# Attention: reciprocal softmax sums of a head turned in one transpose and re-read from memory as rows

## The chip, the cores and the metric

The kernel runs on one core of a Trainium2 chip. The metric is device time in microseconds (us) of one execution, the median of the runs. The core has five engines with queues of their own that run in order: PE (matmuls, and PEld for its weight loads), DVE, ACT, POOL, and SP, which here only issues DMAs. They meet through semaphores; a scheduler places each engine's instructions from the order in which the program issues them and from priorities.

## What is computed

A two-layer trunk over 1024 latent tokens and 256 context tokens. Each layer projects the tokens, runs three token mixers side by side (retention, grouped-query attention GQA with 6 heads, latent attention MLA with 6 heads), multiplies their concatenation by SiLU(gate), and projects back. Only the two attentions and the gate matter here:

```python
def one_block(qi):
    s = jnp.einsum('bqkgd,bskd->bkgqs', qi, k).astype(f32) * scale
    p = jax.nn.softmax(s, axis=-1).astype(v.dtype)
    return jnp.einsum('bkgqs,bskd->bqkgd', p, v)
```

Latent queries see 1536 keys, context queries 256. The kernel does not normalise the probabilities: it multiplies the head's output by the reciprocal of the row sum, and then by the gate.

## The kernel before, in words

The attention of a layer is one list of 60 *pairs*. A pair is (head `i`, token pair `pr`, mixer): 256 tokens of one head of GQA or MLA; pairs 0 to 3 of a head are latent tokens (three key blocks of 512), pair 4 is the context (one key block of 256). GQA runs ahead of MLA by `LEAD` = 3 pairs. Outputs stand transposed: a head's columns `head_cols` in `yxs` hold 64 GQA rows above 64 MLA rows on the partitions, and tokens along the free dimension.

`advance` is one step; in each it issues at most one job of each kind, with lags counted in steps, and `up(...)` gives each kind a priority:

- `s_job`: scores of 128 queries against one key block (PE, L1247, L1248, for MLA also L1250) into a bank "acc"; DVE takes the maximum (L1256).
- `exp_job`: ACT's exponential with the row sum (L1270). After a pair's last block DVE makes the reciprocal sums `ri`, one number for each token, tokens on partitions (L1277, L1278, for the context pair L1280).
- `t_job`: four PE transposes of the probabilities (L1288) into a bank "tp", then ACT rounds (L1292) and DVE takes the rest (L1293). There are two "tp" banks.
- `pv_job`: output matmuls (L1304, L1305) into the only bank "o". When a pair is done ACT copies half of it (L1316) and DVE adds (L1317) into `head_cols`, which releases the bank.
- `y_job`, once both halves of (`i`, `pr`) are done, 30 times a layer: POOL spreads `ri` over 256 columns (`rb`, one buffer, L1355), PE turns it by two transposes into a bank "tp" (L1358), DVE multiplies `head_cols` by that bank (L1359), POOL multiplies by the gate `gt` (L1360). `gt` is loaded by `load_gates` (L1335) when the first half of the pair is done. `gate_retention` (L1344, its load at L1347) gates the retention columns in head 1 and reads a load `gr` with one buffer.

Between the jobs POOL prepares what the next pairs need: `q_piece` splits queries in two terms (L1169, L1171), `qr_piece` the rotary part (L192, L193), and `step` splits the next head's K and V as their loads land (L192, L193). SP issues all loads in order: K and V rows (`st`, L1090, L1107, L1086), rotary queries (`qst`, L1180), gates (L1335).

Of the kernel before, what the change touches and what calls it, by code (L numbers as in the profile page):

```python
# [10 lines left out]
F32 = mybir.dt.float32  # L11
# [3 lines left out]
ALU = mybir.AluOpType  # L15
# [3 lines left out]
P = 128  # L19
# [4 lines left out]
DEPTH = 2  # L24
# [4 lines left out]
Y_H = 256  # L29
# [36 lines left out]
RB = 6  # L66
YV = 1
LEAD = 3
# [8 lines left out]
SV = 0  # L77
WG = 1
PO = 1


def hybrid_trunk(tc, I, O):
# [3 lines left out]
    V, A, G, T = nc.vector, nc.scalar, nc.gpsimd, nc.tensor  # L86
    dma = nc.sync.dma_start
# [6 lines left out]
    s_gT = [tc.dram_tile([D, NT * P], F32, name=f"s_gT{l}") for l in range(DEPTH)]  # L94
# [5 lines left out]
    s_mv = [tc.dram_tile([6 * P, NCH * 64], F32, name=f"s_mv{l}") for l in range(DEPTH)]  # L100
    s_kpT = [tc.dram_tile([NCH * 32, P], F32, name=f"s_kpT{l}") for l in range(DEPTH)]
    s_mt = [tc.dram_tile([P, 512], F32, name=f"s_mt{l}") for l in range(DEPTH)]
    s_gate = [tc.dram_tile([2, D], F32, name=f"s_gate{l}") for l in range(DEPTH)]


    cst = enter(tc.tile_pool(name="cst", reuse_waits="tile", bufs=1))
    wp = enter(tc.tile_pool(name="wp", reuse_waits="tile", bufs=4))
    wr = enter(tc.tile_pool(name="wr", reuse_waits="tile", bufs=1))
    sm = enter(tc.tile_pool(name="sm", reuse_waits="tile", bufs=4))
    pp = enter(tc.tile_pool(name="pp", reuse_waits="tile", bufs=1, space=PSUM))  # L110

    ident = cst.tile([P, P], F32, name="ident")
    dma(ident, I["ident"])
    yxs = cst.tile([P, NT, D], F32, name="yx")
# [19 lines left out]
    def bank(tag):  # L134
        if tag == "o":
            return pp.tile([P, 512], F32, name=tag, tag=tag, bufs=1)
        if tag == "m":
            tag = "tp"
        bufs = {"acc": NACC, "tp": 7 - NACC}[tag]
        return pp.tile([P, 512], F32, name=tag, tag=tag, bufs=bufs)  # L140

    def up(offset):
        return tc.high_priority(offset=offset) if offset else nullcontext()
# [297 lines left out]
    def phase_b(l, p1, acts, ws, first, first_side, first_done, att):  # L441
        pa_ctx = ExitStack()

        def blk(fn, pre=None, post=None, posts=1):
            gran, n = ws.take()
            if pre is not None:
                pre(0)
            for t in range(NT):
                if pre is not None and t + 1 < NT:
                    pre(t + 1)  # L450
                fn(t, project(act_of(acts, t), gran, n))
                if t in (0, 2, 4, 6):
                    ws.pump()
                for _ in range(posts):
                    next(post, None)
# [246 lines left out]
        blk(gqa_fn, post=side)  # L702
        blk(gqb_fn, post=side, posts=PO)
        for _ in side:
# [355 lines left out]
    def attention(l, att):  # L1060
# [3 lines left out]
        at = None  # L1064
# [175 lines left out]
        clock = [0]  # L1240
# [27 lines left out]
        def exp_job(p, i, b, ps):  # L1268
            pn = at.tile([P, 512], F32, name="pn", tag="pn", bufs=PN)[:, :p.w]
            A.activation(pn, ps, AF.Exp, bias=p.ng[i], accum_out=p.su[:, i, b:b + 1])  # L1270
            p.pn[i, b] = pn
            if b == p.nb - 1 and i == 1:
                if (p.i, p.pr) not in ris:
                    ris[p.i, p.pr] = sm.tile([P, 2, 2], F32, name="ri", tag="ri", bufs=RB)
                ri = ris[p.i, p.pr][:, :, p.mla]
                if p.nb > 1:
                    V.tensor_reduce(ri, p.su[:, :, 0:p.nb], axis=AX.X, op=ALU.add)  # L1277
                    V.reciprocal(ri, ri)  # L1278
                else:
                    V.reciprocal(ri, p.su[:, :, 0])  # L1280

        def t_job(p, i, b):
            if i == 0:
                p.gran[b] = at.tile([P, 2, 4, 256], F32R, name="pT", tag="pT", bufs=PT)
            pn = p.pn.pop((i, b))
            pt = bank("tp")
            for c in range(p.nch):
                T.transpose(pt[:, c * 128:(c + 1) * 128], pn[:, c * 128:(c + 1) * 128], ident)  # L1288
            p3 = pt[:, :p.w].rearrange("p (c q) -> p c q", c=p.nch)
            ph = p.gran[b][:, 0, 0:p.nch, i * 128:(i + 1) * 128]  # L1290
            pl = p.gran[b][:, 1, 0:p.nch, i * 128:(i + 1) * 128]
            A.copy(ph, p3)  # L1292
            V.tensor_tensor(pl, p3, ph.bitcast(F32), op=ALU.subtract)  # L1293

        def pv_job(p, b, c0, c1):
            if b == 0 and c0 == 0:
                p.po = bank("o")[:, :256]
            last = p.nb * p.nch - 1
            while (p.i not in MV) if p.mla else p.i // 3 not in GV:
                step(True)  # L1300
            for c in range(c0, c1):
                ch = b * p.nch + c
                vc = (MV[p.i] if p.mla else GV[p.i // 3])[:, p.k0 // 128 + ch, :]
                T.matmul(p.po, vc, p.gran[b][:, 0, c, :], start=(ch == 0), stop=False)  # L1304
                T.matmul(p.po, vc, p.gran[b][:, 1, c, :], start=False, stop=(ch == last))  # L1305
            if b == p.nb - 1 and c1 == p.nch:
                hs = slice(64 * p.mla, 64 * p.mla + 64)
                if YV == 0:
                    o2 = at.tile([P, 2, 256], F32, name="o2", tag="o2", bufs=OH)
                    for u in range(2):  # L1310
                        A.copy(o2[hs, u], p.po[64 * u:64 * u + 64])
                    o4 = o2[hs].rearrange("p a (t c) -> p a t c", t=2)
                    G.tensor_tensor(head_cols(p)[hs], o4[:, 0], o4[:, 1], op=ALU.add)
                else:
                    o2 = at.tile([P, 256], F32, name="o2", tag="o2", bufs=OH)
                    A.copy(o2[hs], p.po[64:128])  # L1316
                    V.tensor_tensor(head_cols(p)[hs], p.po[0:64].rearrange("p (t c) -> p t c", t=2),  # L1317
                                    o2[hs].rearrange("p (t c) -> p t c", t=2), op=ALU.add)
                pairs_done[p.mla] += 1
                halves[p.i, p.pr] = halves.get((p.i, p.pr), 0) + 1  # L1320
                if halves[p.i, p.pr] == 1:
                    load_gates(p)
                else:
                    ys.append((clock[0] + 1, p))

        def head_cols(p):

            return yxs[:, 2 * p.pr:2 * p.pr + 2, Y_H + p.i * 128:Y_H + (p.i + 1) * 128]

        ris, halves, gates = {}, {}, {}  # L1330

        def load_gates(p):

            gates[p.i, p.pr] = g = at.tile([P, 2, 128], F32, name="gt", tag="gt", bufs=LEAD + 1)
            dma(g, s_gT[l][(2 + p.i) * P:(3 + p.i) * P, 2 * p.pr * P:(2 * p.pr + 2) * P].rearrange("p (t c) -> p t c", t=2))  # L1335

        rets = []

# [10 lines left out]

        def y_job(p):  # L1350

            pm = bank("tp")[:, :256]
            ri = ris.pop((p.i, p.pr)).rearrange("p t s -> p (t s)")
            rb = at.tile([P, 256], F32, name="rb", tag="rb", bufs=1)
            G.tensor_scalar(rb.rearrange("p (x c) -> p x c", c=64), ri.unsqueeze(2).to_broadcast([P, 4, 64]), 1.0, 1.0,  # L1355
                            op0=ALU.mult, op1=ALU.mult)
            for i in range(2):
                T.transpose(pm[:, i * 128:(i + 1) * 128], rb[:, i * 128:(i + 1) * 128], ident)  # L1358
            V.tensor_tensor(head_cols(p), head_cols(p), pm.rearrange("p (t c) -> p t c", t=2), op=ALU.mult)  # L1359
            G.tensor_tensor(head_cols(p), head_cols(p), gates.pop((p.i, p.pr)), op=ALU.mult)  # L1360
            gate_retention(p)

        LAG_E, LAG_T, LAG_V = LE, LT, LV
# [1 line left out]
        def advance(jobs):  # L1365

            s = clock[0]
            if jobs is not None:
                with up(OS):
                    s_job(*jobs)  # L1370
            if exps and s >= LAG_E:
                with up(OE):
                    exp_job(*exps.pop(0))
            if trs and trs[0][0] <= s and (trs[0][2], trs[0][3]) in trs[0][1].pn:
                _, p, i, b = trs.pop(0)
                with up(OT):
                    t_job(p, i, b)
                if i == 1:
                    h = max(1, p.nch // HV)
                    pvs.append((s + LAG_V, p, b, 0, h))  # L1380
                    pvs.append((s + LAG_V + 1, p, b, h, p.nch))
            if pvs and pvs[0][0] <= s:
                with up(OV):
                    pv_job(*pvs.pop(0)[1:])
            if ys and ys[0][0] <= s:
                with up(OY):
                    y_job(ys.pop(0)[1])
            clock[0] += 1
# [3 lines left out]
        for x in range(30 + LEAD):  # L1392
            for mla, y in ((1, x - LEAD), (0, x)):
                if 0 <= y < 30:
                    p = Pair()
# [20 lines left out]
        for n, p in enumerate(pairs):  # L1416
# [7 lines left out]
            for u in range(2):  # L1424
                for b in range(p.nb):
                    if early[0] == 0:
                        yield "prepared"
                        at = att.ctx.enter_context(tc.tile_pool(name=f"at{l}", reuse_waits="tile", bufs=1))
# [21 lines left out]
        while exps or trs or pvs or ys:  # L1450
            advance(None)
# [241 lines left out]
```

## Time and profile before

| | us |
|---|---|
| median of 3 runs | 2163.35 (2161.07 to 2163.56) |
| profiled execution, its own time | 2162.85 |
| its span | 2161.1 |
| PE busy in it | 2084.2 (96%) |
| DVE, ACT, POOL busy | 1502.0, 1183.5, 978.2 |

The attention of the first layer fills the trace from about 520 to 998 us, that of the second from about 1562 to 2037 us. A busy share is an average over the whole span, and PE's instructions are pipelined: where PE streams, a row's time from start to start says what an instruction takes; the duration of one row (0.27 us for a single transpose) includes its way through the array.

### The profile page before, as it was taken

To read this page: it belongs to the slowest core of one execution; us is meant where nothing else is said; L and a number is where in the kernel's file an instruction comes from. 1 tells how busy PE (TensorE), PEld (TensorE's weight loads), DVE (VectorE), ACT (ScalarE), POOL (GpSimd) and SP (SyncE) were. 2 spreads that over 40 slices of the span, in tenths; PEclk is the share of its full clock that TensorE was granted. 3 is DMA by queue.
4 is the path that set the end of the run, shared out by engine and by line. 5 is a ranking of instruction groups with operands and counts; after the bars stand their busy time and mean duration, and the time that the engine had idled before them with its cause. 6 is when DMAs were issued, how large, how long until landed. Compare 5 with 4: busy or idle time off the path is not lost. (4 is left out here: it accounts for less than half of the span.)

```text
span 2161.1 us, 42292 instructions
## 1 busy us (share of the span) xinstructions
PE 2084.2 (96%) x14888; PEld 1870.0 (87%) x14888; DVE 1502.0 (70%) x3830; ACT 1183.5 (55%) x3180; POOL 978.2 (45%) x1444
## 2 busy tenths in 40 slices
PE   7999999999999999999999999998999999999998
PEld 3899987788888888888999999887788888888898
DVE  4625583666889999997174358546689899999824
ACT  3503333225788888886243233322488888888623
POOL 2341242315576465533543324233375656453474
PEclk8999999999999999999999999999999999999999
DMA  9542446414111010004143212452311111000322
GB/s 315 145 145 63 123 112 204 122 49 117 36 44 28 20 30 25 13 27 136 46 153 102 66 54 55 140 152 66 109 46 30 32 30 32 14 22 18 98 91 98
DMA packets 189117, 173.30 MB, mean 80 GB/s; under 512 B 35833, under 2 KB 171625, under 8 KB 188905
## 3 DMA queue, kind: packets, MB, share of 16 engines
q1 hardware_dynamic: 187464, 165.35, 25.7%
q10 hardware_dynamic: 1440, 5.24, 0.6%
q8 instruction: 119, 1.95, 0.4%
q14 instruction: 94, 0.76, 0.1%
HBM read 124.77 MB, written 45.76 MB: 79 GB/s over the span
## 5 line engine op out<-in xcount | busy, mean ns | idle before, releaser
L256 PE MATMUL acc<-wh,ah 128*128 128x256 f32 (+1 forms) x1760 | 503.4, 286 | 1.8 <-ACT ah L404 1.8
L258 PE MATMUL acc<-wh,al 128*128 128x256 f32 (+1 forms) x1760 | 500.6, 284 | 2.5 <-DVE al L405 2.4
L257 PE MATMUL acc<-wl,ah 128*128 128x256 f32 (+1 forms) x1760 | 502.7, 286 | 0.0
L1256 DVE TENSOR_REDUCE nm<-acc 128x1 f32<-128x512 f32 (+1 forms) x624 | 411.7, 665 | 39.0 <-PE acc L1250 27.0
L1293 DVE TENSOR_TENSOR pT<-tp,pT 128x512 fp32r<-128x512 f32 (+1 forms) x624 | 413.2, 664 | 36.1 <-ACT pT L1292 30.6
L1292 ACT CAST pT<-tp 128x512 fp32r<-128x512 f32 (+1 forms) x624 | 356.5, 573 | 139.1 <-PE tp L1288 132.8
L1270 ACT ACTIVATE pn<-acc,nm 128x512 f32<-128x512 f32 (+1 forms) x624 | 421.3, 681 | 19.9 <-DVE nm L1261 17.4
L1288 PE MATMUL tp<-ident,pn 128*128 128x128 f32 x2400 | 424.1, 274 | 3.9 <-DVE pT L1293 2.4
L256 PEld LDWEIGHTS acc<-wh,ah 128*128 128x128 f32 x1760 | 334.9, 190 | 13.1 <-issue 8.2
L258 PEld LDWEIGHTS acc<-wh,al 128*128 128x128 f32 x1760 | 332.0, 189 | 5.3 <-DVE al L405 4.5
L257 PEld LDWEIGHTS acc<-wl,ah 128*128 128x128 f32 x1760 | 334.0, 190 | 0.8 <-issue 0.8
L1304 PE MATMUL o<-pT,V 128*128 128x256 f32 x1200 | 326.3, 294 | 0.7 <-DVE yx L1317 0.6
L1288 PEld LDWEIGHTS tp<-ident,pn 128*128 128x128 f32 x2400 | 287.6, 140 | 34.6 <-PE tp L1288 5.8
L1305 PE MATMUL o<-pT,V 128*128 128x256 f32 x1200 | 314.4, 284 | 0.0
L1304 PEld LDWEIGHTS o<-pT,V 128*128 128x128 f32 x1200 | 227.1, 189 | 19.2 <-DVE yx L1317 5.1
L1305 PEld LDWEIGHTS o<-pT,V 128*128 128x128 f32 x1200 | 227.2, 189 | 16.6
L192 POOL TENSOR_SCALAR wh<-raw 128x512 fp32r<-128x512 f32 (+2 forms) x144 | 82.4, 582 | 321.2 <-PE acc L258 143.2
L193 POOL TENSOR_TENSOR wl<-raw,wh 128x512 fp32r<-128x512 f32 (+2 forms) x144 | 164.7, 1155 | 5.2
L1247 PE MATMUL acc<-K,Qm 128*128 128x512 f32 (+1 forms) x312 | 140.6, 451 | 1.0
L683 PE MATMUL acc<-ah,wh 128*128 128x512 f32 (+1 forms) x384 | 141.4, 368 | 0.0
L684 PE MATMUL acc<-ah,wl 128*128 128x512 f32 (+1 forms) x384 | 139.8, 364 | 0.0
L685 PE MATMUL acc<-al,wh 128*128 128x512 f32 (+1 forms) x384 | 139.5, 363 | 0.0
(278 smaller groups left out, 3898.3 us busy)
## 6 DMA issues: line engine op xcount, KB each, us to landing
raw<-in_w_ada_dram SPq DMA_DIRECT2D x96, 256.0 KB, 3.2
raw<-in_w_in_dram SPq DMA_DIRECT2D x56, 256.0 KB, 2.9
kv<-s_rkv SPq DMA_DIRECT2D x40, 256.0 KB, 2.8
s_gT<-eo SPq DMA_DIRECT2D x80, 128.0 KB, 2.2
yx<-in_x_sample_dram SPq DMA_DIRECT2D x16, 512.0 KB, 6.4
gt<-s_gT SPq DMA_DIRECT2D x60, 128.0 KB, 2.1
raw<-in_w_in_dram SPq DMA_DIRECT2D x56, 128.0 KB, 2.5
raw<-in_w_out_dram SPq DMA_DIRECT2D x48, 128.0 KB, 3.0
```

The costliest lines, as they stand in the source:

```text
L193: G.tensor_tensor(wl, raw, wh.bitcast(F32), op=ALU.subtract)
L256: T.matmul(ps, ah[:, k, :], wh, start=(k == 0), stop=False)
L257: T.matmul(ps, ah[:, k, :], wl, start=False, stop=False)
L258: T.matmul(ps, al[:, k, :], wh, start=False, stop=(k == KC - 1))
L683: T.matmul(ps, wh, ah[:, k, :], start=(k == 0), stop=False)
L1256: V.tensor_reduce(nm[:, b:b + 1], ps, axis=AX.X, op=ALU.max, negate=True)
L1270: A.activation(pn, ps, AF.Exp, bias=p.ng[i], accum_out=p.su[:, i, b:b + 1])
L1288: T.transpose(pt[:, c * 128:(c + 1) * 128], pn[:, c * 128:(c + 1) * 128], ident)
L1292: A.copy(ph, p3)
L1293: V.tensor_tensor(pl, p3, ph.bitcast(F32), op=ALU.subtract)
L1304: T.matmul(p.po, vc, p.gran[b][:, 0, c, :], start=(ch == 0), stop=False)
L1305: T.matmul(p.po, vc, p.gran[b][:, 1, c, :], start=False, stop=(ch == last))
```

## The change

For heads 0 to 4 of each layer the reciprocal sums of all five pairs go into one tile `ri` [128, 20]. Two steps (`SL`) after the exponentials of the head's last MLA pair, `store_sums` turns it by one transpose, ACT copies the result (20 x 128), and a DMA stores it to `s_sum`. During the next head, `load_gates` reads each pair's rows back, spread over 64 partitions for each mixer, into `rb` (two buffers), and loads the gate; it is called after the exponentials of MLA pair (`i`+1, `pr`). In `y_job` of (`i`+1, `pr`) POOL multiplies the gate tile by the rows and then the previous head's columns by that. Head 5 has no next head and keeps the old way, with `rb` from the two buffers. `load_gates` is no longer called from `pv_job`.

```diff
             if b == p.nb - 1 and i == 1:
-                if (p.i, p.pr) not in ris:
-                    ris[p.i, p.pr] = sm.tile([P, 2, 2], F32, name="ri", tag="ri", bufs=RB)
-                ri = ris[p.i, p.pr][:, :, p.mla]
+                if p.i not in ris:
+                    ris[p.i] = sm.tile([P, 5, 2, 2], F32, name="ri", tag="ri", bufs=3)
+                ri = ris[p.i][:, p.pr, :, p.mla]
...
+                if p.mla:
+                    if p.i:
+                        load_gates(p.i - 1, p.pr)
+                    if p.i == 5:
+                        load_gates(5, p.pr)
+                    if p.pr == 4 and p.i < 5:
+                        rows_due.append((clock[0] + SL, p.i))
...
-                if halves[p.i, p.pr] == 1:
-                    load_gates(p)
-                else:
+                if halves[p.i, p.pr] == 2:
                     ys.append((clock[0] + 1, p))
...
+        def load_gates(i, pr):
+
+
+            gates[i, pr] = g = at.tile([P, 2, 128], F32, name="gt", tag="gt", bufs=LEAD + 1)
+            dma(g, s_gT[l][(2 + i) * P:(3 + i) * P, 2 * pr * P:(2 * pr + 2) * P].rearrange("p (t c) -> p t c", t=2))
+            if i < 5:
+                srows[i, pr] = rb = at.tile([P, 2, 128], F32, name="rb", tag="rb", bufs=2)
+                rows = s_sum[l][20 * i + 4 * pr:20 * i + 4 * pr + 4, :].rearrange("(t s) q -> s t q", s=2)
+                for s in range(2):
+                    dma(rb[64 * s:64 * s + 64], rows[s:s + 1].to_broadcast([64, 2, 128]))
+
+        def store_sums(i):
+
+            pt = bank("tp")
+            T.transpose(pt[0:20, 0:128], ris.pop(i).rearrange("p r t s -> p (r t s)"), ident)
+            rr = wp.tile([P, 128], F32, name="rr", tag="msb", bufs=1)
+            A.copy(rr[0:20, :], pt[0:20, 0:128])
+            dma(s_sum[l][20 * i:20 * i + 20, :], rr[0:20, :])
...
         def y_job(p):
...
+            if p.i:
+                g, cols = gates.pop((p.i - 1, p.pr)), head_cols(p.i - 1, p.pr)
+                G.tensor_tensor(g, g, srows.pop((p.i - 1, p.pr)), op=ALU.mult)
+                G.tensor_tensor(cols, cols, g, op=ALU.mult)
+            if p.i == 5:
+                pm, cols = bank("tp")[:, :256], head_cols(5, p.pr)
...
             gate_retention(p)
```

On the engines this reads as follows. PE, in the first layer, around the first latent `y_job` of head 2, before (L1358 are the two transposes of `rb`, the L1247 and L1248 rows are scores of the context pair, the L1304 row behind them opens the bank "o" anew):

```order
L1305 MATMUL o<-pT,V 128x256
L1288 MATMUL tp<-ident,pn 128x128 x3
L1247 MATMUL acc<-K,Qg 128x256
L1288 MATMUL tp<-ident,pn 128x128
L1248 MATMUL acc<-K,Qg 128x256
L1247 MATMUL acc<-K,Qg 128x256
L1248 MATMUL acc<-K,Qg 128x256
L1358 MATMUL tp<-ident,rb 128x128 x2
L1304 MATMUL o<-pT,V 128x256
```

and in the change at the same place, where L1247, L1248, L1288, L1304 and L1305 have become L1249, L1250, L1297, L1313 and L1314:

```order
L1314 MATMUL o<-pT,V 128x256
L1297 MATMUL tp<-ident,pn 128x128 x3
L1249 MATMUL acc<-K,Qg 128x256
L1297 MATMUL tp<-ident,pn 128x128
L1250 MATMUL acc<-K,Qg 128x256
L1249 MATMUL acc<-K,Qg 128x256
L1250 MATMUL acc<-K,Qg 128x256
L1297 MATMUL tp<-ident,pn 128x128 x4
L1313 MATMUL o<-pT,V 128x256
```

The two transposes of `rb` are gone, and four transposes of the next `t_job`, which came later, stand in their place ahead of the bank's reopening.

POOL, at the boundary from head 1 to head 2, before (L1355 and L1360 belong to `y_job`, K, Qr, Qg, Qm and V rows are splits):

```order
L193 TENSOR_TENSOR Qr<-qst,Qr 64x256
L1355 TENSOR_SCALAR rb<-ri 128x256
L1169 TENSOR_SCALAR Qg<-yx 64x256 x2
L1171 TENSOR_TENSOR Qg<-yx,Qg 64x256 x2
L1360 TENSOR_TENSOR yx<-yx,gt 128x2x128
L1169 TENSOR_SCALAR Qm<-yx 64x256 x2
L1171 TENSOR_TENSOR Qm<-yx,Qm 64x256
L192 TENSOR_SCALAR V<-st 128x7x64 x2
L193 TENSOR_TENSOR V<-st,V 128x7x64 x2
```

and in the change (L1376 multiplies the gate by the rows, L1377 the columns by that; the splits are two lines further down in the file):

```order
L195 TENSOR_TENSOR Qr<-qst,Qr 64x256
L1171 TENSOR_SCALAR Qg<-yx 64x256 x2
L1173 TENSOR_TENSOR Qg<-yx,Qg 64x256 x2
L1376 TENSOR_TENSOR gt<-gt,rb 128x256
L1377 TENSOR_TENSOR yx<-yx,gt 128x2x128
L1376 TENSOR_TENSOR gt<-gt,rb 128x256
L1377 TENSOR_TENSOR yx<-yx,gt 128x2x128
L1376 TENSOR_TENSOR gt<-gt,rb 128x256
L1377 TENSOR_TENSOR yx<-yx,gt 128x2x128
L1171 TENSOR_SCALAR Qm<-yx 64x256 x2
L1173 TENSOR_TENSOR Qm<-yx,Qm 64x256
L194 TENSOR_SCALAR V<-st 128x7x64 x2
```

Three pairs of head 1 stand in a row ahead of the split of Qm and of V, and the first of them waits for rows that come through memory; the other two pairs follow behind V and Qr.

SP, at the boundary from head 2 to head 3, in the change (`s_sum` is the new store, `rb` the row loads, `gt` gates, `st` K and V rows, `qst` rotary queries):

```order
L1356 DMA s_sum_76<-rr 20x128
L1348 DMA rb<-s_sum_76 64x2x128 x6
L1343 DMA gt<-s_gT_58 128x256
L1348 DMA rb<-s_sum_76 64x2x128 x2
L1343 DMA gt<-s_gT_58 128x256
L1348 DMA rb<-s_sum_76 64x2x128 x2
L1343 DMA gt<-s_gT_58 128x256
L1092 DMA st<-s_mk_68 64x512 x2
L1182 DMA qst<-s_qrT_64 32x2x128 x2
```

The row loads stand behind the store, and the next head's K rows and rotary queries behind the row loads; `rb` has two buffers, so the third pair of row loads comes free when POOL has read the first.

## Rows read from the trace of the kernel before

**Rows 1.** The page, busy time by engine (share of the span, instructions).
```profile
PE 2084.2 (96%) x14888; PEld 1870.0 (87%) x14888; DVE 1502.0 (70%) x3830; ACT 1183.5 (55%) x3180; POOL 978.2 (45%) x1444
```

**Rows 2.** Windows of 60 us: length, busy us (instructions) by engine, granted clock, DMA share, GB/s.
```profile
560.00:620.00 60.00, 57.68 (x391) 51.32 (x390) 51.76 (x110) 47.20 (x121) 37.11 (x61) 0.97 0.11 29
620.00:680.00 60.00, 56.62 (x388) 49.95 (x386) 51.96 (x111) 47.41 (x120) 39.84 (x64) 1.00 0.12 33
680.00:740.00 60.00, 59.81 (x415) 53.05 (x415) 55.00 (x117) 49.46 (x127) 36.44 (x59) 1.00 0.11 30
```

**Rows 3.** PE's timeline at four places: start, duration, instruction, [idle before <-releaser].
```profile
564.80 0.69 PE L1358 MATMUL tp<-ident,rb 128*128 128x128 f32 x2 [2.22 <-POOL rb L1355]
...
647.99 0.44 PE L1358 MATMUL tp<-ident,rb 128*128 128x128 f32 x2 [3.19 <-POOL rb L1355]
...
1604.67 0.44 PE L1358 MATMUL tp<-ident,rb 128*128 128x128 f32 x2 [1.29 <-POOL rb L1355]
...
1686.00 0.44 PE L1358 MATMUL tp<-ident,rb 128*128 128x128 f32 x2 [2.92 <-POOL rb L1355]
```

**Rows 4.** POOL's timeline ahead of two of these places.
```profile
557.88 1.28 POOL L1344 TENSOR_TENSOR yx<-yx,gr 128x512 f32<-128x512 f32 x1 [2.85 <-DMA gr<-s_gT]
...
564.34 0.40 POOL L1355 TENSOR_SCALAR rb<-ri 128x256 f32<-128x256 f32 x1
...
646.44 1.13 POOL L193 TENSOR_TENSOR V<-st,V 128x448 fp32r<-128x448 f32 x1
647.53 0.41 POOL L1355 TENSOR_SCALAR rb<-ri 128x256 f32<-128x256 f32 x1
```

**Rows 5.** Windows of 4 us behind the first place, columns as in rows 2.
```profile
566.00:570.00 4.00, 4.00 (x25) 3.78 (x25) 2.39 (x6) 2.13 (x6) 3.57 (x7) 0.73 0.00 0
```

**Rows 6.** PE's timeline, first y_jobs of heads 2 and 3 (columns as in rows 3).
```profile
725.33 0.49 PE L1288 MATMUL tp<-ident,pn 128*128 128x128 f32 x3
...
725.78 0.27 PE L1288 MATMUL tp<-ident,pn 128*128 128x128 f32 x1
...
726.12 0.28 PE L1248 MATMUL acc<-K,Qg 128*128 128x256 f32 x1
726.48 0.41 PE L1358 MATMUL tp<-ident,rb 128*128 128x128 f32 x2
726.90 0.38 PE L1304 MATMUL o<-pT,V 128*128 128x256 f32 x1
...
805.18 0.41 PE L1358 MATMUL tp<-ident,rb 128*128 128x128 f32 x2
```

**Rows 7.** Who waited for L1317 (first row) and L1359 (second): us, times.
```profile
  PEld o L1304: 5.1, 22
...
  PEld tp L1288: 3.6, 22
```

**Rows 8.** POOL's two y_job lines, and its longest wait between 500 and 1000 us.
```profile
L1355 POOL TENSOR_SCALAR rb<-ri x60: 403/407/411, 564.3 to 2034.4; 128x256 f32<-128x256 f32 x60
L1360 POOL TENSOR_TENSOR yx<-yx,gt x60: 726/735/848, 573.7 to 2037.8; 128x256 f32<-128x256 f32 x60
POOL Qm L1169 <- PE acc L1248: 94.1, 17, 7.4
```

**Rows 9.** Near prices: a small ACT copy; DMA issues (KB, us to landing).
```profile
L1316 ACT COPY o<-o x120: 367/369/373, 534.3 to 2036.3; 64x256 f32<-64x256 f32 x120
s_gT<-eo SPq DMA_DIRECT2D x80, 128.0 KB, 2.2
gt<-s_gT SPq DMA_DIRECT2D x60, 128.0 KB, 2.1
```

**Rows 10.** POOL's timeline at the boundary from head 1 to head 2.
```profile
706.38 0.89 POOL L1169 TENSOR_SCALAR Qm<-yx 64x256 fp32r<-64x256 f32 x2 [3.25 <-PE acc L1248]
```

**Rows 11.** DVE: two lines, duration ns min/median/max.
```profile
L1293 DVE TENSOR_TENSOR pT<-tp,pT x624: 414/681/693, 520.5 to 2033.9; 128x512 fp32r<-128x512 f32 x144, 128x256 fp32r<-128x256 f32 x12
L405 DVE TENSOR_TENSOR al<-yx,ah x44: 418/827/1779, 999.7 to 2058.2; 128x512 fp32r<-128x512 f32 x36, 128x256 fp32r<-128x256 f32 x8
```

More of the change, by code (lines that the diff above doesn't have):

```diff
@@ L79 @@
 PO = 1
+SL = 2
 def hybrid_trunk(tc, I, O):
@@ L102, in hybrid_trunk @@
     s_mt = [tc.dram_tile([P, 512], F32, name=f"s_mt{l}") for l in range(DEPTH)]
+    s_sum = [tc.dram_tile([100, P], F32, name=f"s_sum{l}") for l in range(DEPTH)]
     s_gate = [tc.dram_tile([2, D], F32, name=f"s_gate{l}") for l in range(DEPTH)]
@@ L1312, in pv_job @@
                     o4 = o2[hs].rearrange("p a (t c) -> p a t c", t=2)
-                    G.tensor_tensor(head_cols(p)[hs], o4[:, 0], o4[:, 1], op=ALU.add)
+                    G.tensor_tensor(head_cols(p.i, p.pr)[hs], o4[:, 0], o4[:, 1], op=ALU.add)
                 else:
@@ L1316, in pv_job @@
                     A.copy(o2[hs], p.po[64:128])
-                    V.tensor_tensor(head_cols(p)[hs], p.po[0:64].rearrange("p (t c) -> p t c", t=2),
+                    V.tensor_tensor(head_cols(p.i, p.pr)[hs], p.po[0:64].rearrange("p (t c) -> p t c", t=2),
                                     o2[hs].rearrange("p (t c) -> p t c", t=2), op=ALU.add)
@@ L1320, in pv_job, with head_cols @@
                 halves[p.i, p.pr] = halves.get((p.i, p.pr), 0) + 1
-                if halves[p.i, p.pr] == 1:
-                    load_gates(p)
-                else:
+                if halves[p.i, p.pr] == 2:
                     ys.append((clock[0] + 1, p))
[L1326 to L1335, printed above, removed]
+        def head_cols(i, pr):
+            return yxs[:, 2 * pr:2 * pr + 2, Y_H + i * 128:Y_H + (i + 1) * 128]
+        ris, halves, gates, srows, rows_due = {}, {}, {}, {}, []
+        def load_gates(i, pr):
[12 more added lines that the diff above has]
+            dma(s_sum[l][20 * i:20 * i + 20, :], rr[0:20, :])
         rets = []
@@ L1350, in y_job @@
         def y_job(p):
[L1352 to L1360, printed above, removed]
+            if p.i:
[4 more added lines that the diff above has]
+                pm, cols = bank("tp")[:, :256], head_cols(5, p.pr)
+                rb = at.tile([P, 256], F32, name="rb", tag="rb", bufs=2)
+                G.tensor_scalar(rb.rearrange("p (x c) -> p x c", c=64),
+                                ris[5][:, p.pr].rearrange("p t s -> p (t s)").unsqueeze(2).to_broadcast([P, 4, 64]),
+                                1.0, 1.0, op0=ALU.mult, op1=ALU.mult)
+                for i in range(2):
+                    T.transpose(pm[:, i * 128:(i + 1) * 128], rb[:, i * 128:(i + 1) * 128], ident)
+                V.tensor_tensor(cols, cols, pm.rearrange("p (t c) -> p t c", t=2), op=ALU.mult)
+                G.tensor_tensor(cols, cols, gates.pop((5, p.pr)), op=ALU.mult)
             gate_retention(p)
@@ L1384, in advance @@
                     pv_job(*pvs.pop(0)[1:])
+            if rows_due and rows_due[0][0] <= s:
+                store_sums(rows_due.pop(0)[1])
             if ys and ys[0][0] <= s:
```

## The prediction

> **What bounds the kernel now.** I read the page first: PE is busy 96% of the span, no other engine more than 70% [rows 1], so in most places the time is the sum of what PE has to stream. That is a mean over stages, so next the windows of the attention, where the change sits: in a steady stretch (680 to 740 us) PE is busy 59.81 of 60 us, DVE 55.0, POOL 36.4; in the two windows before it PE loses 2.3 and 3.4 us [rows 2]. The timeline of PE shows where: four `y_job`s, two in each layer, whose transposes find `rb` not yet written. PE then stands idle 2.22, 3.19, 1.29 and 2.92 us, together 9.6 us [rows 3]. POOL's timeline says why `rb` is late: POOL runs in order, and `rb` stands behind a retention gate that had itself waited 2.85 us for its load, or, at the boundary from head 0 to head 1, behind the splits of V [rows 4]. The lists of who waited add two small entries: transposes of probabilities that wait until L1359 has released the "tp" bank (3.6 us, 22 times), and output matmuls that wait for the "o" bank (5.1 us, 22 times) [rows 7].
>
> So two kinds of cost can be saved, PE's own work and PE's waits for `y_job`, and the change adds work to POOL and two trips through memory that nothing on PE consumes directly.
>
> **The change part by part**, against the profiled execution (2162.85 us).
>
> *PE's transposes.* Heads 0 to 4, 5 pairs, 2 layers: 50 `y_job`s lose two transposes each, 100 in all; 10 transposes of `ri` are added. What one costs in a stream: three take 0.49 us where one takes 0.27 [rows 6], so (0.49 - 0.27) / 2 = 0.11 us. 90 x 0.11 = **-9.9 us**. Full price holds only where PE streams on. Where it waits for the "o" bank the transposes filled the wait, and taking them away gives nothing by itself; but the order puts the next four transposes of probabilities there instead. At the first `y_job` of head 2 the scores' last matmul starts at 726.12, the two transposes only at 726.48, the output at 726.90 [rows 6]: 0.78 us for work that streams in about 0.12 + 0.22 = 0.34, so some 0.44 us of waiting, in which four transposes (0.44 us) now fit. Half of that, 0.22 us more than the plain price, at some 6 such places (heads 2 to 4 in both layers; head 3's looks the same) and some remainder at the others: **-1.5 us**, between 0 and -3.
>
> *PE's waits for `rb`.* All four long waits belong to heads 0 and 1, whose `rb` no longer exists: **-9.6 us**. Nothing takes their place at once: the output matmul behind them needs only the bank.
>
> *The clock behind the first wait.* In the window of 566 to 570 us PE is busy throughout at a granted clock of 0.73 [rows 5], in part at the lower level of 1.2 GHz instead of 2.4. That is 4 x 0.27 = 1.1 us, and the piece from 564.8 to 566 us loses about half of itself, 0.6. If PE isn't idle there the clock should not fall: **-1.6 us**; at worst 0, since the longest wait, 3.19 us at 648, lies in a window at a granted 1.00 [rows 2], so the cause is not certain.
>
> *The "tp" bank.* 22 waits of 3.6 us in all go with L1359, for the 50 of 60 `y_job`s that lose it: **-3.0 us** [rows 7]. They are PEld's, so part may be hidden: 0 to -3.
>
> *DVE* loses 50 multiplications. DVE is not the bound here; I take nothing for it.
>
> *ACT* gains ten copies of 20 x 128, each at most the 0.37 us of a 64 x 256 copy [rows 9]; on an engine busy 49 of 60 us that is hidden. The transpose of `ri` needs a "tp" bank until that copy is done, perhaps 0.4 us, ten times; PE has the other bank. Between 0 and +4 us, I take **+0.5**.
>
> *POOL* loses 50 spreads of 0.407 us and gains a second product of about the gate's 0.735 us in each [rows 8]: 50 x (0.735 - 0.407) = +16 us, spread over 10 heads. It has 20 of 60 us free [rows 2], so the sum is hidden; the point is order. At the boundary from head 1 to head 2 the first three pairs of products now stand ahead of the split of Qm, and the first waits for its rows: transpose and ACT copy (0.11 + 0.37), the store (2.2) and the load (2.1, the nearest DMA rows [rows 9]) with their issues, some 5 to 6 us from the transpose. POOL stood idle 3.25 us there [rows 10], so part of the wait falls into idle time. The three pairs are 6 x 0.735 = 4.4 us, all five 7.4 us. Behind them wait the splits of Qm, V and Qr, then SP, whose loads of K, V and rotary queries need buffers that those splits release, and SP also holds the store's and the first rows' waits. Can PE feel it? Queries are split one to two pairs ahead. A head takes 805.18 - 726.48 = 78.7 us [rows 6], so one of its ten pairs 7.9 us, and POOL's commonest wait is for PE to release such a query buffer (94.1 us in 17 times, 5.5 each [rows 8]): it is ahead by that. I expect the delay to be absorbed, except at the boundary from head 0 to head 1, where POOL has no idle time (the splits of V run into `rb` [rows 4]) and PE now arrives earlier by what it gains. There I allow 0 to 3 us in each layer and take **+0.5** each, +1 in all.
>
> *SP* gains 10 stores and 100 row loads; what they hold up is counted under POOL. *Head 5* keeps its work.
>
> Sum: -9.9 - 1.5 - 9.6 - 1.6 - 3.0 + 0.5 + 1.0 = -24.1, so 2138.8 us. The median shown is 0.5 us above the profiled execution, which I leave inside the range. **Forecast 2138.8 us**, 1.1% faster.
>
> **A rule that speaks against it.** L1293, DVE's busiest line here with one operand in PSUM, takes 681 ns in the median and 693 at most, although POOL is busy beside it for over half of the time [rows 2]; L405, with both inputs in SBUF, goes from 418 to 1779 ns [rows 11]. The Trainium skill, page "SBUF — State Buffer", section "Who interferes with whom", says that DVE and GpSimd share a port pair as an exclusive lock, which a DVE instruction with two SBUF inputs contends for with a GpSimd instruction that reads SBUF, while one with at most one SBUF input outside the two-port modes does not. By that rule the added POOL products cost DVE's PSUM operations nothing, and L405's spread, in another phase, would be such blocking; taken more broadly (any two-operand operation of DVE) it would be rival C.
>
> **Rivals.**
> - *A: only the waits go* (the transposes were filling). If PE waited as long for the "o" bank everywhere, the removed transposes would leave idle time. For: 5.1 us of such waits, and rows 6. Against: 22 waits in 60 `y_job`s, and the order fills the place with other transposes. Then -9.6 - 1.6 = -11.2: 2151.7 us.
> - *B: the trip through memory stalls POOL at ten boundaries* (slower). POOL holds at the first product until its rows land, SP holds the next K rows behind the row loads, and the next queries come late. It decides once the delay exceeds the lead of one to two pairs, 8 to 16 us, of which the products take 7.4; so the rows would have to keep POOL another 5 or more. For: queues in order, a store, a load and a two-buffer tile that passes through both. Against: rows 8 and 10. At 5 us a boundary, 10 x 5 = +50 on the forecast: 2188.8 us. Price below about 2 us a boundary and it is still faster.
> - *C: DVE is slowed by POOL's products.* 100 x 0.735 = 73.5 us of POOL products replace 50 gates; if DVE, 55 of 60 us busy, lost half of it, +37: 2175 us. Against: L1293's spread of 12 ns above the median.
> - *D: the order gains more.* If the "o" bank's 5.1 us [rows 7] are hidden by the four transposes that stand there now, and neither of the +1.5 us appears: 2138.8 - 5.1 - 1.5 = about 2132 us.
> - *E: nothing to measure.* The gain is eaten at boundaries at about 2.4 us each, 10 x 2.4 = 24: about 2163 us.
>
> **How the numbers follow.** Forecast 0.55, A 0.18, D 0.11, E 0.07, B 0.06, C 0.03. A measurement tells about 0.2%, 4.3 us, from no change. Faster: forecast, A and D, 0.84; same 0.07; slower B and C, 0.09. Range: D's 2132 less 2 for its own uncertainty, 2130, up to A with 2 us on it for the boundaries, 2154; this leaves out B, C and E, 0.16.
>
> **What would show it.** Right: no PE idle time in front of the output matmuls of `y_job` places in heads 0 and 1, windows 560 to 680 busy above 59.5 of 60, no low clock at 566 us, a head period of about 1 us less in steady state (9 transposes net, 1.0, and the bank), L1293 at 681 ns. Wrong: the transposes of probabilities that now reopen at the "o" bank wait there (A); PE rows that wait for POOL's Qg, Qm, Qr, K or V at the boundaries, with POOL idle on DMA `rb` ahead of L1376 (B, E); L1293 above 700 ns (C). The head period without any change would refute the price of 0.11 us.

## The result

| | before | changed |
|---|---|---|
| median | 2163.45 us (2161.07 to 2165.16, 4 runs) | 2137.75 us (2134.77 to 2141.34, 4 runs) |
| span of the profiled execution | 2161.1 us | 2133.0 us |

The ratio is 0.9881 (95% interval 0.9869 to 0.9894): 1.2% faster. The forecast was 2138.8 us.

The page of the changed kernel, first the engines' rows, to be read beside [rows 1]:

```profile
PE 2064.7 (97%) x14798; PEld 1854.8 (87%) x14798; DVE 1489.9 (70%) x3780; ACT 1177.9 (55%) x3190; POOL 992.8 (47%) x1444
```

PE issues 90 matmuls fewer and is busy 19.5 us less; POOL is busy 14.6 us more (16 were forecast). The three windows of [rows 2] in the changed kernel, with the same columns:

```profile
560.00:620.00 60.00, 59.97 (x413) 52.90 (x414) 54.97 (x116) 50.99 (x133) 36.25 (x57) 1.00 0.08 21
620.00:680.00 60.00, 59.92 (x423) 53.79 (x422) 55.14 (x117) 51.46 (x132) 42.58 (x67) 1.00 0.16 44
680.00:740.00 60.00, 59.90 (x409) 52.71 (x409) 54.45 (x116) 50.17 (x130) 36.84 (x58) 1.00 0.15 43
```

The first two have become like the third: PE streams at a granted 1.00, in the second while POOL is busier than before (42.58 us against 39.84). Not all of the difference of the two spans belongs to the change. I cut each trace at the start of the first score matmul and of the last output matmul of each layer:

```
kernel              start  attention 0  between  attention 1  tail
before              506.5     491.7      549.1      488.8    125.0
changed             503.8     476.9      551.2      476.5    124.5
changed, again      503.2     477.0      552.6      476.8    125.8
```

The two attentions lose 14.8 and 12.3 us, 27.1 in all. Ahead of them 2.7 us are lost and between them 2.1 gained, in code that the change doesn't touch: in the trace of before the granted clock of the first 100 us was 0.91, and 0.95 from 420 to 490 us,

```profile
0.00:100.00 100.00, 83.25 (x589) 56.62 (x590) 52.73 (x164) 52.57 (x134) 26.35 (x34) 0.91 0.73 234
420.00:490.00 70.00, 64.38 (x394) 55.93 (x395) 46.61 (x174) 18.36 (x53) 16.33 (x26) 0.95 0.19 55
```

and in that of the changed kernel 0.95 and 1.00:

```profile
0.00:100.00 100.00, 82.06 (x594) 57.47 (x595) 53.97 (x165) 52.47 (x134) 25.26 (x34) 0.95 0.73 234
420.00:490.00 70.00, 63.84 (x401) 54.58 (x400) 45.98 (x172) 19.45 (x55) 15.28 (x24) 1.00 0.19 57
```

Such differences come and go between executions; so below the sums are made twice, by medians of runs and by the lengths of the attentions (called *attention* below, both layers added, of the one profiled execution of each kernel: 980.5 before, 953.4 changed).

PE's timeline at the first latent `y_job` of head 2, the place of [rows 6]:

```profile
713.63 0.28 PE L1250 MATMUL acc<-K,Qg 128*128 128x256 f32 x1
713.99 0.63 PE L1297 MATMUL tp<-ident,pn 128*128 128x128 f32 x4
714.41 0.39 PE L1313 MATMUL o<-pT,V 128*128 128x256 f32 x1
```

From the last score matmul to the first output matmul it is 0.78 us, as before (726.12 to 726.90). But where two transposes of `rb` stood there are now four transposes of probabilities, which no longer cost their time further down.

POOL's timeline at the boundary from head 1 to head 2, the place of [rows 10]:

```profile
688.43 1.52 POOL L1173 TENSOR_TENSOR Qg<-yx,Qg 64x256 fp32r<-64x256 f32 x2
693.36 0.74 POOL L1376 TENSOR_TENSOR gt<-gt,rb 128x256 f32<-128x256 f32 x1 [3.41 <-DMA rb<-s_sum]
...
697.71 0.74 POOL L1376 TENSOR_TENSOR gt<-gt,rb 128x256 f32<-128x256 f32 x1 [1.29 <-DMA rb<-s_sum]
698.53 0.74 POOL L1377 TENSOR_TENSOR yx<-yx,gt 128x256 f32<-128x256 f32 x1
699.36 0.88 POOL L1171 TENSOR_SCALAR Qm<-yx 64x256 fp32r<-64x256 f32 x2
```

The first product does wait for its rows, with the split of Qm queued behind it. The answer on line L1376 gives all such waits together, those on L1348 the loads' time from issue to landing:

```profile
L1376 POOL TENSOR_TENSOR gt<-gt,rb x50: 723/737/747, 621.2 to 1990.8; 128x256 f32<-128x256 f32 x50
...
  DMA rb<-s_sum: 46.2, 17
```

```profile
DMA to landing us min/median/max: 2.6/2.7/3.9
```

POOL stood 46.2 us for rows, in 17 waits, and no instruction of PE, DVE or ACT waits for L1376 or L1377 (SP's loads wait for the buffers that they free). A row load takes 2.7 us, not the 2.1 that a gate's load took before.

### The profile page after: what moved, and what is told of

Same layout as the page of the kernel before. It is cut to its first block, busy times and chain, and to the rows that moved or that the text cites. A ratio compares the mean times of both kernels' runs of the same rounds, so it can differ in the third digit from the quotient of the medians.

```text
span 2133.0 us, 42211 instructions
## 1 busy us (share of the span) xinstructions
PE 2064.7 (97%) x14798; PEld 1854.8 (87%) x14798; DVE 1489.9 (70%) x3780; ACT 1177.9 (55%) x3190; POOL 992.8 (47%) x1444
## 5 line engine op out<-in xcount | busy, mean ns | idle before, releaser
L1297 PE MATMUL tp<-ident,pn 128*128 128x128 f32 x2400 | 433.6, 274 | 3.9 <-DVE pT L1302 2.3
L1302 DVE TENSOR_TENSOR pT<-tp,pT 128x512 fp32r<-128x512 f32 (+1 forms) x624 | 412.7, 663 | 27.8 <-ACT pT L1301 19.4
L1313 PE MATMUL o<-pT,V 128*128 128x256 f32 x1200 | 326.2, 293 | 1.5 <-DVE yx L1326 1.5
L1297 PEld LDWEIGHTS tp<-ident,pn 128*128 128x128 f32 x2400 | 287.5, 140 | 35.9 <-PE acc L1250 7.4
L1314 PE MATMUL o<-pT,V 128*128 128x256 f32 x1200 | 312.1, 282 | 0.0
L1313 PEld LDWEIGHTS o<-pT,V 128*128 128x128 f32 x1200 | 226.6, 189 | 19.9 <-DVE yx L1326 6.0
L1314 PEld LDWEIGHTS o<-pT,V 128*128 128x128 f32 x1200 | 226.4, 189 | 17.8
L1249 PE MATMUL acc<-K,Qm 128*128 128x512 f32 (+1 forms) x312 | 143.3, 459 | 0.0
L1250 PE MATMUL acc<-K,Qm 128*128 128x512 f32 (+1 forms) x312 | 138.7, 444 | 0.0
```

The source lines that it names most:

```text
L1249: T.matmul(ps, p.Q[:, 0, qs], K, start=True, stop=False)
L1250: T.matmul(ps, p.Q[:, 1, qs], K, start=False, stop=not p.mla)
```

## The experiments

**Transposes put back.** The changed kernel, with two transposes of a constant in the `y_job`s of heads 0 to 4:

```diff
+            if p.i < 5:
+                px = bank("tp")[:, :256]
+                for i in range(2):
+                    T.transpose(px[:, i * 128:(i + 1) * 128], ident, ident)
```

> The changed kernel with two transposes of a constant put back into each y_job of heads 0 to 4 (100 in all), into a tp bank that nobody reads. If the transposes stream on PE at 0.11 us each (my theory), they cost about 11 us: 2149 us, ratio to the kernel before 0.993. If they only filled waits (rival A) they cost 0 to 2 us: 2138 to 2140 us, ratio 0.988 to 0.989.

Measured 2153.93 us, ratio to before 0.9958 (0.9946 to 0.9971): +16.2 us on the changed kernel, attention +18.6. Rival A is out, and the plain price of 0.11 us each is too low by some 5 us in all. PE's wait list for the transposes of probabilities names a new entry there:

```profile
  PE tp L1381: 5.9, 20
```

The next transposes wait for the added ones to leave the bank. So I moved these to another bank:

```diff
-                px = bank("tp")[:, :256]
+                px = bank("acc")[:, :256]
```

> The run that put 100 transposes back cost 16 us, not 11: 10.9 us of streaming and some 5 to 8 us of small waits. Here the same transposes write an acc bank (five in rotation) in place of a tp bank (two in rotation). If the small waits come from the tp rotation (a transpose of probabilities finds its bank taken by the added ones): about 11 us over the changed kernel, 2149 us, ratio 0.9935. If they come from the place in PE's order: 2154 us as before, ratio 0.996.

Measured 2148.55 us, ratio 0.9934 (0.9922 to 0.9947): +10.8 us on the changed kernel, 0.108 us for each of 100 transposes (attention +12.3, so 0.12). The entry of 5.9 us has become 0.6, in the list of who waited for the added transposes:

```profile
L1381 PE MATMUL acc<-ident x100: 270/272/329, 559.4 to 1967.1; 128*128 128x128 f32 x100
...
  PEld tp L1297: 0.6, 4
```

A price of 0.11 to 0.12 us is shown; the other 5.4 us (6.3 by attention) go with the choice of bank. (Nobody reads it here, so its next writer waits for PE itself; the scheduler's order differs a little too.)

**DVE's product too.** The first run's edit, and DVE multiplies the columns by the bank (by that constant):

```diff
+                hc = head_cols(p.i, p.pr)
+                V.tensor_tensor(hc, hc, px.rearrange("p (t c) -> p t c", t=2), op=ALU.mult)
```

> As the run before, and DVE multiplies the head's columns by that bank, as L1359 did, so the bank is held. Theory: 3 us more for the waits on the tp bank, about 2152 us, ratio 0.995, so that what is left against the kernel before is the waits for rb and the clock (11 us). If the bank's waits are hidden: the same as the run before.

Measured 2155.14 us, ratio 0.9965 (0.9952 to 0.9977): +1.2 on the first run, whose interval overlaps (attention +2.7). A miss in its size: once the transposes take a bank, that DVE reads it adds little. To before 7.4 us are left, not 11, but this run holds what the change added as well.

**Waits taken away from the kernel before.**

```diff
-                T.transpose(pm[:, i * 128:(i + 1) * 128], rb[:, i * 128:(i + 1) * 128], ident)
+                T.transpose(pm[:, i * 128:(i + 1) * 128], rb[:, i * 128:(i + 1) * 128] if p.i > 1 else ident, ident)
```

> The kernel before, whose transposes in heads 0 and 1 read a constant instead of rb (POOL still writes rb; nothing else changes, so the multiplication is by the wrong numbers there). Theory: the four long waits (9.6 us) and the low clock behind the first (1.6 us) go and nothing takes their place: 2152 us, ratio 0.995. Rival: the same work of POOL is waited for a little later (Qg or V behind rb), and less than 5 us is gained: above 2158 us.

Measured 2152.19 us, ratio 0.9951 (0.9939 to 0.9964): -10.4 us by medians, attention -9.7. At the first place of [rows 3] PE's timeline now reads

```profile
559.32 0.28 PE L1248 MATMUL acc<-K,Qg 128*128 128x256 f32 x1
559.68 0.41 PE L1358 MATMUL tp<-ident 128*128 128x128 f32 x2
560.10 0.39 PE L1304 MATMUL o<-pT,V 128*128 128x256 f32 x1
```

The 2.22 us are gone, and the same 0.78 us from the last score matmul (559.32) to the first output matmul (560.10) stands there as at head 2. In the kernel before it was 3.66 us at the second place of [rows 3], around the wait of 3.19 us:

```profile
644.53 0.28 PE L1248 MATMUL acc<-K,Qg 128*128 128x256 f32 x1
...
648.19 0.36 PE L1304 MATMUL o<-pT,V 128*128 128x256 f32 x1
```

So that wait is worth 2.88 us, its length less about 0.3 us that lay under it; the same 0.3 us is found at the third and the fourth place. Nothing came in their place.

**The "tp" bank in the kernel before.**

```diff
-            pm = bank("tp")[:, :256]
+            pm = bank("acc")[:, :256]
```

> The kernel before, with the transposes of rb in all y_jobs into an acc bank in place of a tp bank, and nothing else changed. This prices the tp bank alone, which the prediction put at 3.0 us, and which the runs with transposes put back suggest to be about 5: 2158 us, ratio 0.9975. If the acc banks are as tight, 0 or a loss.

Measured 2164.97 us, ratio 1.0013 (1.0005 to 1.0022): no gain, rather a small loss (attention +1.3). By the lists of who waited, the outputs wait less for DVE's add (3.9 us against 5.8), the scores more for the exponentials (11.2 against 8.2), and the transposes of probabilities in all about as long as before (20.5 against 19.8), though none of it is for L1359 any more. The four long waits for `rb` have grown too, from 9.6 us to 11.4, which is more than the loss by attention. So moving the load to the other banks moves the wait, and even without the longer waits for `rb` the bank alone would not be worth the 3.0 us that I gave it. One more thing is seen in its trace, at the first place of [rows 3] again, PE's timeline and the window of 20 us behind it:

```profile
562.53 0.44 PE L1358 MATMUL acc<-ident,rb 128*128 128x128 f32 x2 [2.83 <-POOL rb L1355]
```

```profile
560.00:580.00 20.00, 17.32 (x121) 15.50 (x122) 15.24 (x35) 13.54 (x36) 14.78 (x25) 1.00 0.06 17
```

A longer idle time than the 2.22 us of before, and the clock stays at 1.00. It fell elsewhere in this execution, in part to the lower level of 1.2 GHz, behind the fourth of these waits:

```profile
1686.93 0.44 PE L1358 MATMUL acc<-ident,rb 128*128 128x128 f32 x2 [3.24 <-POOL rb L1355]
```

```profile
1688.00:1692.00 4.00, 4.00 (x22) 3.69 (x21) 2.16 (x6) 2.89 (x9) 3.57 (x7) 0.62 0.10 33
```

**The trip through memory.** The changed kernel without the store, its rows read from memory written long before:

```diff
-            dma(s_sum[l][20 * i:20 * i + 20, :], rr[0:20, :])
...
-                rows = s_sum[l][20 * i + 4 * pr:20 * i + 4 * pr + 4, :].rearrange("(t s) q -> s t q", s=2)
+                rows = s_gT[l][20 * i + 4 * pr:20 * i + 4 * pr + 4, 0:P].rearrange("(t s) q -> s t q", s=2)
```

> The changed kernel without the store, the rows read from other memory that is written long before (the gate rows stand in, so the normalisation is left out). POOL then waits for no store. Theory: the trip through memory is hidden, 0 plus or minus 2 us against the changed kernel: 2136 to 2140 us. If the trip costs PE something at the boundaries (a mild form of rival B): faster by 3 us or more.

Measured 2136.33 us, ratio 0.9877 (0.9862 to 0.9892), attention +0.7 on the changed kernel. The trip costs nothing that can be told. POOL still waited there, now for the gate's load, so this run takes away the dependence on the store, not all waiting.

**More work on POOL, two doses.** In the changed kernel the product by the rows is issued n times:

```diff
-                G.tensor_tensor(g, g, srows.pop((p.i - 1, p.pr)), op=ALU.mult)
+                rr = srows.pop((p.i - 1, p.pr))
+                for _ in range(3):
+                    G.tensor_tensor(g, g, rr, op=ALU.mult)
```

> The changed kernel with the product of gate and rows issued three times (the result is a wrong power of the rows): 2 x 5 x 0.737 = 7.4 us more of POOL at each head boundary, 74 us in all. Theory: POOL's lead of one to two pairs (8 to 16 us) absorbs it, 0 to 4 us, at most 2142 us. Rival B in its general form (PE already stands near POOL's limit): 10 x 7.4 = 74 us less what is idle, 2170 us or more.

Measured 2138.03 us, ratio 0.9883 (0.987 to 0.9897): 7.4 us more at every boundary are absorbed but for a rest that the medians don't show (attention +2.8). With `range(7)`:

> The same product seven times: 6 x 5 x 0.737 = 22 us more of POOL at each head boundary. Theory: this exceeds the lead of 8 to 16 us, so PE waits 6 to 14 us at each boundary of the ten: 2200 to 2280 us. If POOL has more room than that (its idle time at a boundary is spread so that all fits): below 2160 us.

Measured 2175.79 us, ratio 1.0056 (1.004 to 1.0072): +38 us (attention +39.9), slower than before, though less than the 2200 expected. PE's timeline names the place, the boundary from head 0 to head 1, and who it waits for:

```profile
656.48 0.79 PE L1249 MATMUL acc<-K,Qg 128*128 128x512 f32 x1 [8.67 <-POOL Qg L1171]
```

In the run with three products the same place shows the first touch:

```profile
650.67 0.50 PE L1250 MATMUL acc<-K,Qg 128*128 128x512 f32 x1 [0.97 <-POOL Qg L1173]
```

This is the end of rival B's chain, queries that come late, brought about by POOL's work and not by the trip. Its threshold differs by boundary: from head 0 to head 1 it lies just below 7.4 us of added POOL work, at the others between 7.4 and 22. PE's waits for POOL's queries come to 28.1 us in the run with seven products, 16.9 of them in one wait a layer at that boundary; the granted clock falls to 0.50, the level of 1.2 GHz, behind it as well, here in the first layer:

```profile
656.50:660.00 3.50, 2.93 (x9) 2.33 (x10) 0.69 (x1) 0.04 (x1) 3.20 (x5) 0.50 0.00 0
```

The DVE line that rival C was about shows no effect of the 221 us of extra POOL products either:

```profile
L1302 DVE TENSOR_TENSOR pT<-tp,pT x624: 411/680/695, 516.9 to 2047.0; 128x512 fp32r<-128x512 f32 x144, 128x256 fp32r<-128x256 f32 x12
```

**Two attempts to do better.** The changed kernel with `NACC = 4`, so four "acc" banks and three "tp":

> The changed kernel with one bank moved from acc (five, now four) to tp (two, now three). If the remaining small waits of the transposes on their bank decide (15 us in the trace), it gains up to 8 us: 2130 us. If the scores' banks are as tight, it loses as much: 2145 us.

Measured 2174.64 us, ratio 1.0051 (1.0039 to 1.0064): +37 us (attention +41.4). The line of the scores' first matmul waits for the exponentials that release "acc",

```profile
  ACT pn L1272: 34.0, 112
```

where the same entry is 3.9 us in 6 waits in the changed kernel. Last, with five banks, the remaining transposes of sums moved from "tp" to "acc" (`pm` in `y_job` of head 5, `pt` in `store_sums`), and the changed kernel timed again beside it:

> The changed kernel with what is left of such transposes (head 5's, and the one of a head's sums) in an acc bank. If each such use of a tp bank costs about 0.1 us, 20 of them in all: 2 us less at most, 2135.7 us, at the edge of what can be told.

> The changed kernel itself beside the others of this call: 2137.75 us again, within 2 us.

Measured 2135.85 us, ratio 0.9879 (0.9864 to 0.9893), against 2137.15 us, 0.9882 (0.9868 to 0.9896): not to be told apart (attention 0.9 less).

**Head by head.** An attention of a layer has 600 of the matmuls L1304 (L1313 in the changed kernel), 100 for each head. From every hundredth of them to the next, in the first layer, in us:

```
kernel                        head to head
before                        83.51  81.59  78.79  78.71  78.95
waits for rb taken away       80.03  78.75  78.83  78.74  79.02
changed                       78.79  77.03  77.07  77.41  77.04
transposes back in "acc"      79.48  78.22  78.26  78.61  78.31
transposes back in "tp"       79.54  78.89  78.91  79.23  78.87
products issued 3 times       78.83  78.51  77.02  77.37  77.05
products issued 7 times       78.81  89.03  79.03  79.14  81.04
```

The first two steps hold the waits for `rb`. In the other three the changed kernel is 1.3 to 1.9 us shorter. Ten transposes a head put back in "acc" give back 1.2 us of it (0.12 each), and put back in "tp" all of it: every step is then within 0.5 us of the kernel whose waits were taken away, and three of the five within 0.2. So where no wait for `rb` stands, the gain is these transposes and their turn in "tp", and little is left for anything else.

## Why the prediction was right, step by step

- *Waits for `rb` and the clock:* forecast -9.6 and -1.6, together -11.2. Measured -10.4 (attention -9.7, of it 6.2 in layer 0 and 3.5 in layer 1). The four waits count about 1 us less than their length, for what lay under each. The low clock was priced about right: layer 0 gives 2.7 us more than layer 1, of which the waits explain 1.2 (5.41 against 4.21), so some 1.5 us went to the low clock in that execution. But it doesn't belong to that wait. In the run with the "acc" bank the clock stayed at 1.00 behind 2.83 us at the same place and fell behind the 3.24 us wait of layer 1. In each of these two profiled executions it fell behind one of the four waits; whether it does in others, no run shows.
- *Transposes:* forecast -9.9 for 90. The transposes put back in "acc" cost 0.108 us each by medians, 0.12 by attention, so -9.7 to -11.1.
- *Order, "tp" bank and new costs:* forecast -1.5, -3.0 and +1.5, together -3.0. What is left between the run without the waits and the changed kernel is 2152.19 - 2137.75 = 14.4 by medians, less 9.7 gives -4.7; by attention 17.4, less 11.1 gives -6.3. So the three together are worth more than forecast, and their division isn't shown. At head 2 the order did what was said, four transposes in the place of two, but no run prices the order by itself. The "tp" term had the wrong step in it: it priced the wait for DVE's read of the bank (3.6 us), and DVE's read adds only 1.2 us (attention 2.7), while the transposes' own turn in "tp", for which the sum had no term, is worth 5.4 us (6.3) in the changed kernel. In the order of before a move of the bank alone gained nothing (1.0013).
- *New costs by themselves:* of the +1.5, the +0.5 for the bank that the copy of the sums holds is seen in the changed kernel's trace, as waits of the next transposes for ACT's L1355:

```profile
  PEld tp L1297: 1.9, 10
```

These are waits of weight loads, which may be hidden in part; the run that moved this transpose to "acc" gained too little to be told. The +1.0 for the boundaries isn't seen: POOL's wait for rows is real (46.2 us) and the lead covers it; the lead is smallest where it was expected, from head 0 to head 1. SP's row loads held up nothing that PE needed. Still the new costs aren't nothing: the run with transposes and DVE's product put back does all that the run without the waits does, and the change's new work besides, and takes 3.0 us longer (attention 3.9; the intervals overlap a little), of which the ten transposes of sums are some 1.1. The rest isn't divided.

- *The signs named:* the windows from 560 to 680 us are above 59.5, no low clock stands at 566, L1302 is at 680 ns. The head period fell by 1.3 to 1.9 us where about 1 was expected, since the turn in "tp" comes on top of the streaming.
- *Rival D:* output matmuls and their weight loads still wait for the "o" bank in the changed kernel (L1326, DVE's add), no less than the 5.1 us of before, so its extra gain isn't there:

```profile
  PEld o L1313: 6.0, 17
...
  PE o L1313: 1.5, 3
```

- *DVE:* L1302 stays at 680 ns, in the changed kernel too. The rule of the Trainium skill, page "SBUF — State Buffer", section "Who interferes with whom", agrees as far as it goes here: this instruction has one SBUF input, and it is not slowed. No run here adds POOL work beside L405, with its two, so that half isn't tested.

That the sum came out within 1.1 us is in part luck: waits and clock were 0.8 us too large (1.5 by attention), order, bank and new costs 1.7 too small (3.3), and the two errors cancel. By attention alone the gain is 27.1 us, 3 more than forecast.

## What to carry to other kernels

On an engine that streams, a short helper instruction costs its streaming time (here 0.11 to 0.12 us, not the 0.27 of its row) and its turn in every rotation that it passes through, so look for what writes the same banks. A wait that ends late on an in-order engine is worth its length less whatever lies under it, which a neighbouring place without the wait shows. Work that is moved to an engine off the path is free up to that engine's lead over the path; a dose on the chip measures the lead, place by place, better than its idle share does (POOL was idle some 20 of 60 us; 22 us more in a head of 77 cost 12 at the boundary from head 0 to head 1, and 2 to 4 at the others).

## What was not expected

An idle time of 2.22 us was followed by a window at 0.73 in one execution [rows 5], while 2.83 us at the same place in another was not, and 3.24 us later in that one was: the clock's fall doesn't follow from the length of the idle time alone. And moving one bank from "acc" to "tp" cost 37 us, nearly half as much again as all of this change gains.
